# Block 2's first modulation on VectorE during attention, and two norms from one pass of squares

## The chip, the core and the metric

The kernel runs on one core of a Trainium2 chip. A core has a matrix engine (TensorE: PE for matmuls, PEld for its weight loads), a vector engine (VectorE, DVE), an engine for functions of one operand (ScalarE, ACT), a general engine (GpSimd, POOL) and a queue engine (SyncE, SP). DMA transfers are issued on the queues of SP and POOL. The metric is the time of one execution on the device, in microseconds (us).

## What is computed

Two transformer blocks, one after the other, on 512 tokens of width 1024, and 256 context tokens for each. All in float32.

Block 1 (`first_block`, one layer): a modulation from a conditioning vector; a mixer of differential attention (4 heads) and gated linear attention (GLA, 4 heads, forward and backward); then a mixture of experts, 32 experts with two per token. It ends with a norm.

Block 2 (`second_block`, two layers): for each layer a modulation, neighbourhood attention, a gated branch, latent attention, a merge, and a feed-forward part; the context rows go through all of layer 0, and through the keys and values of layer 1. What the change touches:

```python
x = x + gt2 * hier_moe(...)                 # block 1: the experts are added
return rms_norm(x, final_norm_g)            # end of block 1
...
s_c = silu(c); s_ctx = silu(c_ctx)          # block 2
for i in range(2):
    mod = s_c @ w_mod[i] + b_mod[i]         # 1024 x 6144, for the latent rows
    mod_c = s_ctx @ w_mod[i] + b_mod[i]     # the same matrix, for the context rows
    ...
    h  = rms_norm(x, g_norm1[i]) * (1 + sc1) + sh1
    hc = rms_norm(ctx, g_norm1[i]) * (1 + mc[1]) + mc[0]
```

So block 1's last norm is followed directly by block 2's first: two root-mean-square norms behind each other on the same rows.

## The kernel before

Rows lie transposed: eight tiles of 128 features by 512 tokens (256 for context). Nearly all products are done in three passes: every weight chunk of 128x1024 is loaded (`wr`), split into a high part on ACT (`wh`, line 168) and a low part on DVE (`wl`, line 169), and multiplied as high x high, high x low, low x high (lines 193 to 195).

The program is written as generators that yield a cost after each step. `Stream` counts cost divided by its speed, and `weave` takes the next step from the stream with the least count, until its main streams are done; streams in `back` go along. The order in which steps are emitted is a priority: a planner then sets the order of instructions on each engine and queue, and an engine works its own list in order. Buffers come from tags with a fixed number of tiles (line 22): `t2` 35 of 512 columns, `wa` 14 and `raw` 4 of 1024, `hl` 6, `at` 9 of 768.

`run` goes through these stages. The times are those of the profiled execution.

- `front`, 0 to 420 us: block 1's norm, projections, GLA and attention. GLA (`gla`, from about 155 us) is woven with gates, values and the first head's projection. In the back goes `mods`, block 1's own second and third modulation group. Then each head `attend(hd)` is woven with the projection `qk(hd + 1)` of the next one; the fourth begins at about 377 us.
- The fourth head also has `ctx` in the back: block 2's work for the context rows of layer 0, `path(0, 256)`. It begins with `opening`, the first of three groups of layer 0's modulation; the second and third (`later`) run beside it and are drained ahead of `gains(..., 2)`.
- `project` (output projection, to about 545 us), with `ctx` at speed 0.3; `route` (norm, router, slots; to about 612 us), at 0.5.
- `experts`, 612 to 1400 us: 16 pairs, each 13.1 of cost (three yields of 4.2 and one of 0.5), with `ctx` at `CTX_SPEED` 1.65. Weight tiles `we` come on SP's queue, the context path's `wr` on POOL's.
- `combine`, from 1400 us, `ctx` at the same speed: gathers each token's two expert rows, adds them to X (line 1064), takes squares (`stat`: ACT and DVE in turn, POOL adds them up), sums over features by matmuls with ones (`rms`, line 249), takes the reciprocal root in twelve small DVE steps (`rsqrt`), spreads it (`spread`), scales X (line 1072), stores it, and takes squares of the scaled X for the next norm.
- `drain(weave(ctx))`, then `path(0, 512)`: its first norm (`norm_mod`, lines 267 to 280) takes those squares, and the rest of block 2 follows, until the end.

A modulation group in `mods_group` (line 312 on) loads 32 tiles of 128x512 of the matrix and multiplies each with both conditioning vectors in a 128x32 operand (line 327). It then copies the sum, transposes it and adds the bias. Both vectors are served by one matmul.

## Time and profile before

| | us |
|---|---|
| median of 3 runs | 3503.2 (3502.89 to 3504.28) |
| the profiled execution, its own time | 3501.3 |
| its span, first to last instruction | 3499.5 |
| PE busy | 3328.7 (95%) |
| DVE busy | 1692.5 (48%) |
| ACT busy | 1235.7 (35%) |
| POOL busy | 420.9 (12%) |
| mean granted TensorE clock | 0.975 |

Busy shares are of the span. A PE that is busy is not PE at its peak. In the page's slices a digit is the busy share in tenths, and PEclk the granted TensorE clock in tenths of full speed (2.4 GHz; the lower level is 1.2 GHz). In a table by stretch, "44.08 (x120)" is 44.08 us busy with 120 instructions.

### The profile page before, as it was taken

To read this page: it belongs to the slowest core of one execution; us is meant where nothing else is said; L and a number is where in the kernel's file an instruction comes from. 1 tells how busy PE (TensorE), PEld (TensorE's weight loads), DVE (VectorE), ACT (ScalarE), POOL (GpSimd) and SP (SyncE) were. 2 spreads that over 40 slices of the span, in tenths; PEclk is the share of its full clock that TensorE was granted. 3 is DMA by queue.
4 is the path that set the end of the run, shared out by engine and by line. 5 is a ranking of instruction groups with operands and counts; after the bars stand their busy time and mean duration, and the time that the engine had idled before them with its cause. 6 is when DMAs were issued, how large, how long until landed. Compare 5 with 4: busy or idle time off the path is not lost. (4 is left out here: it accounts for less than half of the span.)

```text
span 3499.5 us, 48890 instructions
## 1 busy us (share of the span) xinstructions
PE 3328.7 (95%) x19280; PEld 2520.3 (72%) x19280; DVE 1692.5 (48%) x3173; ACT 1235.7 (35%) x2194; POOL 420.9 (12%) x558
## 2 busy tenths in 40 slices
PE   7999998999999999599999999999999999999998
PEld 4987556665666666596577777888797777778887
DVE  5336545434333333544356746444645466554443
ACT  4214323333323332233344523333334344433332
POOL 1000022112221221300001021000300001010000
PEclk9999999999999999799999999999999999999999
DMA  7341566898899999335731232333433222132332
GB/s 264 90 130 37 192 228 246 325 333 322 333 377 357 380 371 343 138 99 181 242 97 50 68 109 85 109 126 96 145 98 108 81 68 67 43 109 96 97 97 78
DMA packets 197076, 596.03 MB, mean 170 GB/s; under 512 B 32124, under 2 KB 36988, under 8 KB 196845
## 3 DMA queue, kind: packets, MB, share of 16 engines
q1 hardware_dynamic: 157148, 463.36, 38.3%
q0 software_dynamic: 39696, 129.54, 10.4%
q8 instruction: 152, 2.49, 0.3%
q14 instruction: 80, 0.65, 0.1%
HBM read 563.69 MB, written 33.29 MB: 171 GB/s over the span
## 5 line engine op out<-in xcount | busy, mean ns | idle before, releaser
L169 DVE TENSOR_TENSOR wl<-wr,wh 128x1024 fp32r<-128x1024 f32 (+2 forms) x452 | 554.9, 1229 | 570.3 <-ACT wh L168 541.8
L168 ACT ACTIVATE wh<-wr 128x1024 fp32r<-128x1024 f32 (+2 forms) x452 | 473.8, 1049 | 723.5 <-PE mm L194 546.6
L193 PE MATMUL mm<-wh,h 128*128 128x256 f32 (+1 forms) x1104 | 321.1, 291 | 6.6 <-ACT h L278 4.9
L194 PE MATMUL mm<-wl,h 128*128 128x256 f32 (+1 forms) x1104 | 317.7, 288 | 0.0
L195 PE MATMUL mm<-wh,h 128*128 128x256 f32 (+1 forms) x1104 | 317.1, 288 | 0.3 <-DVE h L279 0.2
L193 PE MATMUL mm<-u,wh 128*128 128x512 f32 (+1 forms) x768 | 274.2, 357 | 4.3 <-ACT wh L168 4.2
L193 PE MATMUL mm<-f,wh 128*128 128x512 f32 (+1 forms) x768 | 274.4, 359 | 3.6 <-ACT f L278 3.2
L194 PE MATMUL mm<-f,wh 128*128 128x512 f32 (+1 forms) x768 | 273.6, 357 | 0.0
L195 PE MATMUL mm<-u,wl 128*128 128x512 f32 (+1 forms) x768 | 272.6, 355 | 0.7 <-DVE wl L169 0.7
L195 PE MATMUL mm<-f,wl 128*128 128x512 f32 (+1 forms) x768 | 273.1, 356 | 0.0
L194 PE MATMUL mm<-u,wh 128*128 128x512 f32 (+1 forms) x768 | 272.7, 355 | 0.0
L1020 PE MATMUL gu<-we,xT 128*64 128x512 f32 x1024 | 239.4, 599 | 0.2 <-ACT xT L165 0.2
L193 PEld LDWEIGHTS mm<-wh,h 128*128 128x128 f32 x1104 | 215.9, 196 | 19.5 <-issue 7.3
L195 PEld LDWEIGHTS mm<-wh,h 128*128 128x128 f32 x1104 | 215.0, 195 | 8.4 <-issue 6.4
L194 PEld LDWEIGHTS mm<-wl,h 128*128 128x128 f32 x1104 | 215.9, 196 | 4.8 <-issue 4.0
L193 PE MATMUL pg<-h,wh 128*128 128x512 f32 (+1 forms) x576 | 213.1, 370 | 6.4 <-ACT th L1723 3.8
L194 PE MATMUL pg<-h,wh 128*128 128x512 f32 (+1 forms) x576 | 208.7, 362 | 0.0
L195 PE MATMUL pg<-h,wl 128*128 128x512 f32 (+1 forms) x576 | 208.4, 362 | 0.0
L356 ACT ACTIVATE p<-S,mx 128x768 f32<-128x768 f32 (+2 forms) x192 | 144.5, 755 | 104.9 <-DVE mx L1429 61.4
L193 PEld LDWEIGHTS mm<-u,wh 128*128 128x128 f32 x768 | 145.9, 190 | 32.0 <-issue 7.5
L193 PEld LDWEIGHTS mm<-f,wh 128*128 128x128 f32 x768 | 146.1, 191 | 31.8 <-issue 6.5
L1020 PEld LDWEIGHTS gu<-we,xT 128*64 128x64 f32 x1024 | 71.4, 137 | 129.1 <-issue 121.4
(513 smaller groups left out, 6538.5 us busy)
## 6 DMA issues: line engine op xcount, KB each, us to landing
we<-in_expert_w_gate_dram SPq DMA_DIRECT2D x128, 512.0 KB, 9.5
we<-in_expert_w_up_dram SPq DMA_DIRECT2D x128, 512.0 KB, 11.4
we<-in_expert_w_down_dram SPq DMA_DIRECT2D x128, 512.0 KB, 11.0
wr<-in_ffn_w_dram SPq DMA_DIRECT2D x128, 512.0 KB, 3.7
wr<-in_w_in_dram SPq DMA_DIRECT2D x120, 512.0 KB, 4.0
wr<-in_ffn_w_dram POOLq DMA_DIRECT2D x64, 512.0 KB, 6.9
wr<-in_w_in_dram POOLq DMA_DIRECT2D x58, 512.0 KB, 4.5
wm<-in_w_mod_dram SPq DMA_DIRECT2D x96, 256.0 KB, 4.9
```

Of the source, the lines that this page charges most:

```text
L168: self.nc.scalar.activation(hi, src, AF.Copy)
L169: self.nc.vector.tensor_tensor(lo, src, hi.bitcast(F32), op=OP.subtract)
L193: mm(out, ah, bh, start=i == 0, stop=False)
L194: mm(out, ah, bl, start=False, stop=False)
L195: mm(out, al, bh, start=False, stop=i == n - 1)
L356: self.nc.scalar.activation(p, s, AF.Exp, bias=m, accum_out=sm)
L1020: nc.tensor.matmul(gu[64 * e:64 * e + 64, m * 512:m * 512 + 512], xT[k // 4][:, o:o + 64], w[e][kk], start=k == 0, stop=k == KD - 1)
```

## The change

Layer 0's modulation of block 2 leaves TensorE. `mods2_cols` loads the matrix transposed (`w_mod_t`, laid out on the host; 48 column blocks of 128, in two halves of 512 inputs) and both conditioning vectors as rows repeated on all partitions (`c2_rows`). It makes four rows of silu and computes each column by two multiply-and-sum instructions for each vector on DVE. It is a stream `cols` in the back of GLA and of the first three heads, and is drained ahead of the fourth. `ctx` is then `path(0, 256)` alone, and starts in the fourth head at speed 1.0 (`LAST_SPEED`; 0.5 before); its speed is 1.45 in the experts (1.65 before) and 2.0 in `combine` (1.65 before).

`combine` takes squares of X and of X times the gain `gf`, both on ACT, sums all sixteen tiles by matmuls, and computes both reciprocal roots r and r2 from these sums. X is not scaled there. `path(0, 512)` multiplies its gain by `gf`, norms the unscaled X with r2, and then (`normed`) scales and stores X. What is left of `ctx` is no longer drained ahead of `path(0, 512)` but woven with its first norm.

```diff
-CTX_SPEED = 1.65
+CTX_SPEED = 1.45
+TAIL_SPEED = 2.0
+COL_COST = 2.0
+LAST_SPEED = 1.0
...
     def rms(self, st, n):
         acc, T = self.tp("ss"), n // P
-        for t in range(T):
+        self.sums(acc[:, :T], st)
+        return self.rsqrt(acc[:, :T], T, 1.0 / D)
+
+    def sums(self, acc, st):
+        for t in range(acc.shape[1]):
             for i, sq in enumerate(st):
-                self.nc.tensor.matmul(acc[:, t:t + 1], sq[:, t * P:(t + 1) * P], self.ones[:, :1], start=i == 0, stop=i == 1)
+                self.nc.tensor.matmul(acc[:, t:t + 1], sq[:, t * P:(t + 1) * P], self.ones[:, :1], start=i == 0, stop=i == len(st) - 1)
...
-            later = Stream(rest(), 1.0, False)
-            ctx = [Stream(chain(opening(), self.path(0, 256, before=later))), later]
+            ctx = [Stream(self.path(0, 256))]
         for s in ctx:
-            s.speed = 0.5
+            s.speed = LAST_SPEED
...
-                                     (self.experts(), CTX_SPEED, False), (self.combine(), CTX_SPEED, False)):
+                                     (self.experts(), CTX_SPEED, None), (self.combine(), TAIL_SPEED, None)):
...
-            drain(weave(ctx))
+            self.rest = ctx
...
+        cols = Stream(self.mods2_cols(0, COL_COST) if ctx else iter(()), 1.0, False)
+        drain(weave([Stream(gla(), 1.0, False), Stream(chain(gates(), dv(), qk(0)), 1.2)], [mods, cols]))
         drain(mods.gen)
         for hd in range(4):
+            if hd == 3:
+                drain(cols.gen)
             drain(weave([Stream(attend(hd), 1.0, False), Stream(chain(gate_norm() if hd == 0 else (), qk(hd + 1) if hd < 3 else ()), 1.2)],
-                        ctx if hd == 3 else ()))
+                        ctx if hd == 3 else [cols]))
...
     def combine(self):
...
-            self.stat(ss, m, X[m], 512)
+            for sq, g in ((ss, 1.0), (sg, gf[:, m:m + 1])):
+                sq.append(self.t2("sq"))
+                nc.scalar.activation(sq[-1], X[m], AF.Square, scale=g)
+            yield 1
         del Y
+        acc = self.tp("ss")
+        self.sums(acc[:, :4], ss)
+        self.sums(acc[:, 4:8], sg)
+        yield 1
+        keep = self.t2("keep")
+        r, v, r2 = (keep[:, 4 * i:4 * i + 4] for i in range(3))
+        nc.vector.tensor_copy(r, self.rsqrt(acc[:, :4], 4, 1.0 / D))
+        nc.vector.tensor_tensor(v, r, r, op=OP.mult)
+        nc.vector.tensor_tensor(v, v, acc[:, 4:8], op=OP.mult)
+        nc.vector.tensor_tensor(r2, self.rsqrt(v, 4, 1.0 / D), r, op=OP.mult)
         yield 4
-        r = self.spread(self.rms(ss, 512), 512)
-        yield 8
-        ss = []
+        self.norms = gf, r, r2
+
+    def normed(self, X, norm):
+        nc, (gf, r, _) = self.nc, self.norms
+        yield from norm
+        r = self.spread(r, 512)
         for m in range(KD):
             nc.vector.scalar_tensor_tensor(X[m], X[m], gf[:, m:m + 1], r, op0=OP.mult, op1=OP.mult)
             nc.gpsimd.dma_start(self.xs_dram[0][m], X[m])
-            self.stat(ss, m, X[m], 512)
-            yield 1.5
-        self.ss = ss
+            yield 0.7
...
+    def mods2_cols(self, L, cost):
+        nc = self.nc
+        bt, mod = self.mod2[L]
+        rows = [[self.load(self.at("crow")[:, :512], self.A["c2_rows"][c, h]) for h in range(2)] for c in range(2)]
+        junk = self.t2("junk")
+        for s in rows[0] + rows[1]:
+            nc.scalar.activation(junk, s, AF.Tanh, scale=0.5)
+            nc.vector.scalar_tensor_tensor(s, junk, 1.0, s, op0=OP.add, op1=OP.mult)
+        yield 1
+        for j in range(48):
+            w = [self.load(self.at("wc")[:, :512], self.A["w_mod_t"][j, h]) for h in range(2)]
+            for c in range(2):
+                to, beg = mod[:, j, c:c + 1], bt[:, j:j + 1]
+                for h in range(2):
+                    nc.vector.tensor_tensor_reduce(junk, w[h], rows[c][h], 0.5, beg, OP.mult, OP.add, to)
+                    beg = to
+            yield cost
...
+            if L == 0:
+                nc.vector.tensor_tensor(m["a1"], m["a1"], self.norms[0], op=OP.mult)
+                r = self.norms[2]
...
+        if L == 0 and lat:
+            norm = self.normed(X, norm)
...
+        if L == 0 and lat:
+            norm = chain(weave([Stream(norm, 1.0, False)], self.rest), weave(self.rest))
         yield from norm
...
-        if before:
-            yield from before.gen
...
-    A["w_mod"] = np.stack([modw(x["w_mod_2"][i]) for i in range(2)])
+    A["w_mod"] = modw(x["w_mod_2"][1])
+    A["w_mod_t"] = ca(x["w_mod_2"][0].T.reshape(48, P, 2, 512).transpose(0, 2, 1, 3))
+    A["c2_rows"] = ca(np.repeat(np.stack([x["c_2"][0], x["c_ctx_2"]]).reshape(2, 2, 1, 512), P, 2))
```

## Rows read from the trace of the kernel before

**Rows 1.** The page, its parts 1 and 2 (busy times; 40 slices).
```profile
PE 3328.7 (95%) x19280; PEld 2520.3 (72%) x19280; DVE 1692.5 (48%) x3173; ACT 1235.7 (35%) x2194; POOL 420.9 (12%) x558
...
PE   7999998999999999599999999999999999999998
...
PEclk9999999999999999799999999999999999999999
```

**Rows 2.** Busy time by stretch: length, engines (instructions), PEclk, DMA share, GB/s.
```profile
155.00:272.00 117.00, 115.43 (x856) 94.12 (x855) 44.08 (x120) 23.41 (x50) 3.71 (x4) 1.00 0.36 113
272.00:377.00 105.00, 101.24 (x555) 78.56 (x554) 70.34 (x118) 46.78 (x94) 8.41 (x6) 0.98 0.10 31
377.00:420.00 43.00, 41.05 (x189) 21.03 (x188) 24.50 (x58) 14.17 (x32) 1.86 (x2) 0.92 0.73 242
420.00:545.00 125.00, 120.77 (x482) 60.26 (x480) 53.67 (x121) 28.07 (x44) 22.09 (x29) 0.99 0.73 255
545.00:612.00 67.00, 58.53 (x373) 44.48 (x372) 43.56 (x154) 26.26 (x43) 18.80 (x31) 0.95 0.66 236
612.00:1400.00 788.00, 774.71 (x4855) 503.12 (x4856) 307.87 (x586) 265.30 (x494) 161.83 (x255) 0.99 0.93 349
1400.00:1465.00 65.00, 30.21 (x167) 26.51 (x165) 35.88 (x65) 14.20 (x18) 33.91 (x37) 0.65 0.48 172
```

**Rows 3.** Tile mod alone, 377 to 612 us: busy; one matmul; its loads (min/median/max ns).
```profile
sum 235.00, PE 74.66 PEld 10.10 DVE 2.05; mean PE 24.89 PEld 3.37 DVE 0.68
...
468.56 1.04 PE L327 MATMUL mod<-wm,mod2ss 128*32 128x512 f32 x2
...
L152 SPq DMA_DIRECT2D wm<-in_w_mod_dram x144: 327/328/1339, 377.1 to 1738.3; - x144
```

**Rows 4.** Groups by line: instructions, count | busy us, mean ns | idle before.
```profile
L169 DVE TENSOR_TENSOR dqk<-rx,dqk 128x512 fp32r<-128x512 f32 x8 | 5.5, 685 | 1.2 <-ACT dqk L168 1.2
L711 DVE TENSOR_REDUCE hss<-sq 128x4 f32<-128x512 f32 x4 | 2.5, 673 | 0.0
L169 DVE TENSOR_TENSOR wl<-wr,wh 128x1024 fp32r<-128x1024 f32 x16 | 19.5, 1222 | 6.6 <-ACT wh L168 6.6
...
L1057 DVE SCALAR_TENSOR_TENSOR yr<-yr,cc,yr x4: 1276/1278/1284, 1410.3 to 1422.0; 128x1024 f32<-128x1024 f32 x4
...
L356 ACT ACTIVATION_READ_ACCUMULATOR p<-S,mx 128x1 f32 x192 | 38.2, 199 | 0.0
```

**Rows 5.** PE's waits, 1397 to 1480 us: total, times, longest; two instructions.
```profile
PE ss L249 <- POOL sq L242: 19.1, 2, 13.3
PE rb L209 <- DVE rs L222: 5.0, 2, 2.5
...
1415.28 0.48 DVE L1396 SCALAR_TENSOR_TENSOR xr<-mm,cc,xr 128x256 f32<-128x256 f32 x1 [1.07 <-PE mm L195]
...
452.81 0.50 PE L249 MATMUL ss<-cc,sq 128*128 128x1 f32 x4
```

**Rows 6.** Timeline, 1427 to 1465 us: start, length, engine, instruction [idle before].
```profile
1432.06 0.74 DVE L1064 SCALAR_TENSOR_TENSOR xr<-yT,cc,xr 128x512 f32<-128x512 f32 x1
...
1436.32 3.57 PE L249 MATMUL ss<-cc,sq 128*128 128x1 f32 x16 [5.83 <-POOL sq L242]
...
1443.62 2.06 DVE L1072 SCALAR_TENSOR_TENSOR xr<-xr,cc,rb 128x512 f32<-128x512 f32 x3 [1.35 <-PE rb L209]
...
1456.80 3.57 PE L249 MATMUL ss<-cc,sq 128*128 128x1 f32 x16 [13.29 <-POOL sq L242]
...
1464.02 2.06 DVE L271 SCALAR_TENSOR_TENSOR nt<-xr,cc,rb 128x512 f32<-128x512 f32 x3 [1.27 <-PE rb L209]
```

**Rows 7.** The experts' matmuls (groups by line), and the stretch with most DMA.
```profile
L1020 PE MATMUL gu<-we,xT 128*64 128x512 f32 x1024 | 239.4, 599 | 0.2 <-ACT xT L165 0.2
...
L1039 PE MATMUL py<-we,hT 128*64 128x512 f32 x512 | 116.0, 601 | 0.1
...
1250.00:1300.00 50.00, 49.94 (x319) 32.39 (x316) 17.77 (x26) 16.70 (x28) 8.79 (x14) 1.00 0.99 377
```

More of the change, by code (lines that the diff above doesn't have):

```diff
@@ L379, in run @@
         if two:
-            place = lambda n: self.place(n)
-            first = Stream(self.mods2(0, "t2", (0,), place))
-            def rest():
-                while not first.done:
-                    yield 1
-                yield from self.mods2(0, "t2", (1, 2), place)
-            def opening():
-                while not first.done:
-                    yield first.step()
-            later = Stream(rest(), 1.0, False)
-            ctx = [Stream(chain(opening(), self.path(0, 256, before=later))), later]
+            ctx = [Stream(self.path(0, 256))]
         for s in ctx:
-            s.speed = 0.5
+            s.speed = LAST_SPEED
         if two and not one:
@@ L409, in run @@
                     s.speed = speed
-                drain(weave([Stream(gen, 1.0, held, (lambda: tc.high_priority(PRIOR)) if PRIOR and held is not None and speed != CTX_SPEED else None)], ctx))
+                drain(weave([Stream(gen, 1.0, bool(held), (lambda: tc.high_priority(PRIOR)) if held is not None else None)], ctx))
         if two:
-            drain(weave(ctx))
+            self.rest = ctx
             self.fill = [Stream(self.path(1, 256), FILL_SPEED)]
@@ L728, in gate_norm @@
             yield 0.5
-        mods = Stream(chain(*[self.mods_group(mod, s0, A["w_ada"], g, "at", lambda n: self.place(n)) for g in (1, 2)]), MOD_SPEED, False)
-        self.place = self.dd
-        drain(weave([Stream(gla(), 1.0, False), Stream(chain(gates(), dv(), qk(0)), 1.2)], [mods]))
+        mods = Stream(chain(*[self.mods_group(mod, s0, A["w_ada"], g, "at", self.dd) for g in (1, 2)]), MOD_SPEED, False)
+        cols = Stream(self.mods2_cols(0, COL_COST) if ctx else iter(()), 1.0, False)
+        drain(weave([Stream(gla(), 1.0, False), Stream(chain(gates(), dv(), qk(0)), 1.2)], [mods, cols]))
         drain(mods.gen)
-        self.place = self.mm
         for hd in range(4):
+            if hd == 3:
+                drain(cols.gen)
             drain(weave([Stream(attend(hd), 1.0, False), Stream(chain(gate_norm() if hd == 0 else (), qk(hd + 1) if hd < 3 else ()), 1.2)],
-                        ctx if hd == 3 else ()))
-        self.place = self.dd
+                        ctx if hd == 3 else [cols]))
         def project():
@@ L1045, in combine @@
     def combine(self):
-        nc, ss = self.nc, []
+        nc, ss, sg = self.nc, [], []
         X = self.X = self.load_x(self.xs_dram[0], 512, "xr", "wa")
@@ L1163, in second_start @@
         self.mod2 = [self.mods(A["b_mod"][L], f"mod2{L}") for L in range(2)]
+    def mods2_cols(self, L, cost):
[15 more added lines that the diff above has]
+            yield cost
     def mods2(self, L, tag, groups=range(3), place=None):
         for g in groups:
-            yield from self.mods_group(self.mod2[L], self.s2, self.A["w_mod"][L], g, tag, place)
+            yield from self.mods_group(self.mod2[L], self.s2, self.A["w_mod"], g, tag, place)
     def gains(self, L, c, half):
@@ L1177, in gains, with path @@
                     b2=self.col(mod, 3, c, "b2" + pre), g2=self.col(mod, 5, c, "g2" + pre))
-    def path(self, L, n, side=None, before=None):
+    def path(self, L, n, side=None):
         nc, A = self.nc, self.A
@@ L1191, in path @@
             X, self.X = self.X, None
-            r = self.ss
+            if L == 0:
+                nc.vector.tensor_tensor(m["a1"], m["a1"], self.norms[0], op=OP.mult)
+                r = self.norms[2]
+            else:
+                r = self.ss
         else:
```

1 line of the change is left out of this document (removed).

## The prediction

> **What bounds the kernel now.** The page comes first: TensorE (PE) is busy for 95% of the span, VectorE (DVE) for 48%, and of the slices of PE only one is far below nine tenths, the seventeenth, where PEclk falls too [rows 1]. So this kernel is a queue of matrix work. What shortens it is matrix work taken away or a hole closed; what lengthens it is anything that makes PE wait. The next view cuts the span at the places that the change touches [rows 2]. To be seen there: 155 to 377 us (the gated linear attention, then the first three heads) and 612 to 1400 us (the experts, with block 2's context rows woven in) have PE busy for 96% or more. From 1400 to 1465 us (the combination of the experts) it is busy for 30.2 of 65 us at a granted clock of 0.65. DVE has room between 155 and 272 us (44.1 of 117) and less between 272 and 377 us (70.3 of 105). DMA engines are busy for 0.36 and 0.10 of those two stretches, and for 0.93 of the experts' stretch.
>
> **What the modulation costs today.** Layer 0's three groups are 96 matmuls in 192 records, and between 377 and 612 us they hold PE for 74.7 us [rows 3]. They go one by one, each about 1.04 us for its two records [rows 3], because each waits for its own 256 KB. All of that goes. Its 96 loads don't go: they move ahead, from this stretch into 155 to 377 us, still on SP's queue, at 0.33 us of issue each [rows 3], with four loads of rows added. They bring 25 MB into stretches with 0.10 to 0.36 DMA share, which hides them. On SP's queue, which is in order, the projections' weight loads stand behind them; a load that waits for a buffer holds these up. That cost is in the second rival.
>
> **What the modulation costs afterwards.** 48 columns x 2 vectors x 2 halves = 192 multiply-and-sum instructions of 128x512 on DVE, and four small preparations. The trace has no such instruction. Lower bound: the plain product of two 128x512 tiles, 0.685 us [rows 4]. Near row above it: ScalarE's read-out of a sum takes 0.2 us more [rows 4], so 0.885 if the sum is read out the same way. Upper bound: product and separate sum, 0.685 + 0.673 = 1.36 us [rows 4]. I take 0.80, between the first two, since a product that streams one element at a time can add as it goes.
>
> By the code's own step costs the columns take 1 + 48 x 2 = 97 units: the linear attention's stretch gives about 56 units (27 columns), the three heads 15 each (the other 21). DVE's spare time there is (117 - 44.1) + (105 - 70.3) = 107.6 us [rows 2]. The columns ask for 192 x 0.80 = 154 us. PE's work in both stretches is unchanged and has nothing to give, so the excess is paid in time: **192 x d - 107.6 = +46 us** at d = 0.80; +24 at 0.685; +153 at 1.36. The excess could also vanish: block 2's path is now allowed from the fourth head on, and DVE has 18 us to spare in 377 to 420 and 71 in 420 to 545 [rows 2]; if columns slide there, it falls towards zero. I don't count on it, since they are emitted ahead of the fourth head.
>
> The Trainium skill has a rule against this step: "Vector Engine (DVE) Microarchitecture Reference", section "Points that are easy to get wrong", says that the instruction form with two sources and an accumulator halves its throughput when both sources are in SBUF and not bf16. The nearest row disagrees as far as it goes: scalar_tensor_tensor of two 128x1024 f32 tiles in SBUF takes 1.28 us, the plain product of that size 1.22 [rows 4]; but it sums nothing. By the page, an estimate of d is 0.685 + (1.222 - 0.685) = 1.22 us, the excess 127 us, and the time some 3534 us.
>
> **The hole behind the experts.** After the last context matmul (its result at 1415.3 us) PE waits: 19.1 us for POOL's additions of squares, 5.0 us for the two reciprocal roots [rows 5]. The chain is: additions to X until 1432.8, POOL's adds of squares, sums from 1436.3, root, X scaled from 1443.6, a second set of squares with POOL's adds, sums from 1456.8, root, norm at 1464.0 [rows 6]. Afterwards there are no POOL adds and no second pass: last X, its two squares on ACT, the remaining sums, a root, three small steps, a second root with the spread. A root with its spread takes 3.7 us (1439.9 to 1443.6 [rows 6]), so the norm could start about 1444, 20 us sooner, if PE has the sums' time free. The scaling of X and its eight stores come behind the norm, beside matmuls, where DVE and POOL have room; I cost them at nothing, and at 8 x 2.06 / 3 = 5.5 us [rows 6] if they block DVE's splits.
>
> The larger part is what fills the hole. The context path's steps sum to 403 units. Before: 50 units until the experts begin (its first group of modulation aside), 346 in them (16 x 13.1 x 1.65), 8 in the combination. Now: 15.7 (fourth head) + 13.4 (projection) + 31.8 (routing) = 61, then 16 x 13.1 x 1.45 = 304, leaving 38 units for the combination and the norm. A unit is worth (774.7 - 239.4 - 116.0) / 346 = 1.2 us of PE [rows 2, 7]. So 46 us of matrix work lands where PE now idles for 34.8 us [rows 2], and the same amount less lies in the experts' stretch (42 x 1.2 = 51 us, of which 13 us moved ahead). Work that is only moved changes nothing; what is won is the idle time. I count 25 of 34.8 (10 stay, at the gathers and the roots) and 8 for the clock: 30.2 us of work at a granted 0.65 would be 20 at full clock [rows 2], two of the ten left in doubt: **-33 us**, bounds -43 and 0.
>
> The sums cost PE more: 128 records where 32 stood (16 before each norm), at 0.50 / 4 = 0.125 us [rows 5]: **+12 us**; +21 at the half clock's 3.57 / 16 = 0.22 [rows 6].
>
> **Sum.** -74.7 + 46 - 33 + 12 = -50 us on the span of 3499.5: 3450; with the 1.8 us around the span (3501.3) and the 1.9 by which the median is above the profiled execution, **3453 us**.
>
> **Rivals.**
> 1. *Slower: the multiply-and-sum takes two passes.* For: nothing in the trace sums while it multiplies on DVE, a reduction of 128x512 alone costs as much as the product [rows 4], and the heads' DVE is already 67% busy. Against: the 1.28 us row. Gains are 74.7 + 33 - 12 = 96 us, so the point of decision is 192 d - 107.6 = 96, d = 1.06 us. At d = 1.36 the time is 3453 + 107 = 3560. The page's rule above falls here as well (3534). Chance 0.15.
> 2. *The heads choke on buffers.* Tag "at" has nine; the four rows of the conditioning vectors hold four until the last column, two go to each column, and three are left: one query tile's two p and its pt. Then tiles no longer overlap, and each of a tile's five DVE steps can stand behind one 0.8 us multiply: 12 x 5 x 0.8 = 48 us more, 3501 us. For: nine buffers now let three tiles overlap. Against: tiles follow each other at 105 / 12 = 8.75 us with DVE two thirds busy, so much of a step's wait for DVE is in that time already. Chance 0.13.
> 3. *The experts' weights can't come faster.* That stretch moves 349 GB/s x 788 us = 275 MB [rows 2] and would shrink to 737 us; the 268 MB left to it (42 of 403 units of the path's 63 MB, 122 loads of 512 KB, lie outside) need 364 GB/s. The best 50 us reached 377 [rows 7], but the mean was 349. If 355 is the limit, 755 us, +18: 3471. Chance 0.12.
> 4. *The hole stays.* If the order puts context work ahead of the combination after all, the 33 us don't come: 3486. Chance 0.08.
>
> **How the numbers follow.** The forecast has 0.52, for its own range of 3420 to 3490. Other cases: 0.15 at about 3560, 0.13 at 3501, 0.12 at 3471, 0.08 at 3486. Low end: d = 0.685 (+24), hole -43, gives 3421; a spill of the columns into later room takes away most of that 24: 3405. High end 3530: above it lies most of rival 1 (0.13, with d from about 1.2 on), and a few hundredths lie below 3405. 0.2% of 3503 is 7 us, what can be told from no change: faster means under 3496, slower over 3510. Faster: 0.52 + 0.12 + 0.08 less 0.02 of tails = 0.70. Same: most of rival 2, 0.10. Slower: rival 1, the rest of rival 2 and a tail, 0.20.
>
> **What would show it.** Right: no mod matmul ahead of the experts but block 1's own; the fourth head starting some 46 us later than 377, with DVE near nine tenths busy and PE below it ahead of that; multiply-and-sum at 0.7 to 0.9 us; the first expert matmul at about 612 - 75 + 46 + 14 = 597; context matmuls of the feed-forward part between the combination's transposes and a granted clock near 1 there; the norm of block 2 within 50 us of the last expert. Wrong: a multiply-and-sum above 1.06 us; waits of the heads' ACT or PE for a freed "at" buffer; experts' matmuls waiting for "we" loads; PE idle behind the experts as now.

## The result

The changed kernel takes **3523.6 us** (median of 5 runs, 3519.5 to 3525.5) where the kernel before took 3503.2 (5 runs on the same chip): a ratio of 1.0054, 95% interval 1.0042 to 1.0066. It is half a per cent slower; 3453 was forecast. The profiled execution has a span of 3521.8 us, at a mean granted clock of 0.967 (before: 0.975).

Page of the changed kernel, parts 1 and 2 (the slices are 88 us each):

```profile
PE 3332.4 (95%) x19172; PEld 2556.9 (73%) x19172; DVE 1813.0 (51%) x3552; ACT 1241.3 (35%) x2206; POOL 406.4 (12%) x546
...
PE   7998879899999999899999999999999999999998
...
PEclk9999979899999999899999999999999899999999
```

Beside [rows 1]: the seventeenth slice, the hole behind the experts, has gone from 5 to 8 tenths of PE and from 7 to 8 of the clock, so it is mostly filled, as forecast. New are three lower slices, the fourth to the sixth (264 to 528 us), with the clock at 7 tenths in the sixth. Something was won where it was expected, and something was lost in attention.

The busy time by stretch, cut at landmarks: the first score matmul of attention, the last maximum of head 4, the first norm of the routing, the first expert matmul, the last one, the first norm of block 2. The columns are stretch, length, then busy time of PE, weight loads, DVE, ACT, POOL with instructions, granted clock, DMA share, GB/s. First the kernel before, three of these stretches:

```profile
150.00:272.60 122.60, 120.95 (x898) 99.06 (x898) 46.62 (x127) 25.03 (x53) 3.71 (x4) 1.00 0.36 113
272.60:418.80 146.20, 140.49 (x733) 98.80 (x736) 93.22 (x173) 60.19 (x123) 10.27 (x8) 0.96 0.28 92
1394.30:1464.00 69.70, 35.91 (x211) 31.64 (x207) 36.69 (x65) 15.92 (x19) 35.54 (x40) 0.68 0.48 170
```

The changed kernel, all six:

```profile
150.00:320.40 170.40, 164.57 (x909) 103.25 (x907) 110.42 (x320) 25.15 (x53) 3.64 (x4) 1.00 0.58 182
320.40:517.50 197.10, 158.12 (x744) 123.50 (x745) 170.17 (x409) 65.61 (x135) 18.88 (x20) 0.80 0.31 98
517.50:607.90 90.40, 82.65 (x477) 70.72 (x477) 52.98 (x109) 31.10 (x46) 24.09 (x33) 0.96 0.56 181
607.90:685.40 77.50, 65.64 (x410) 54.48 (x410) 50.29 (x173) 38.10 (x74) 17.43 (x27) 0.87 0.61 218
685.40:1406.50 721.10, 710.05 (x4396) 447.30 (x4397) 270.53 (x512) 230.09 (x429) 147.27 (x231) 1.00 0.96 368
1406.50:1485.30 78.80, 70.05 (x476) 67.17 (x473) 39.30 (x73) 31.84 (x45) 19.18 (x26) 0.83 0.51 170
```

Read as lengths, with those of before at the same landmarks:

| stage | before | after | difference |
|---|---|---|---|
| up to the first score matmul | 272.6 | 320.4 | +47.8 |
| four heads | 146.2 | 197.1 | +50.9 |
| projection | 123.0 | 90.4 | -32.6 |
| routing | 73.5 | 77.5 | +4.0 |
| experts | 779.0 | 721.1 | -57.9 |
| combination, to block 2's norm | 69.7 | 78.8 | +9.1 |
| the rest | 2035.5 | 2036.5 | +1.0 |

**Up to the end of the heads 98.7 us are lost; behind them 76.4 are won.** The prediction's steps, sorted in the same way: +46 for VectorE's excess, -16 for the mod matmuls that leave head 4 (PE 16.1 us on tile mod from 272.6 to 418.8 us before) and +13 for context work that moves ahead into it make +43 ahead; -93 is left behind. The first half was 56 us short, and the experiments are mainly about that; the second was 17 short.

Three views of the changed kernel name suspects. The multiply-and-sum itself, by line (count, busy us, mean ns), is not one of them: 192 of 0.765 us, the second line overlapping the first, and 148.4 us of DVE time together (72.3 of it ahead of the first score matmul, 76.1 in the heads), so d = 0.77 where 0.80 was forecast.

```profile
L1190 DVE CUSTOM_DVE_ANT_0 junk<-wc,crow,cc 128x512 f32<-128x512 f32 x192 | 146.8, 765 | 5.2 <-DMA wc<-in_w_mod_t_dram 4.1
L1190 DVE DVE_READ_ACCUMULATOR2_ANT cc<- 128x1 f32 x192 | 15.7, 82 | 0.0
```

The second view is tile mod. Block 1's own modulation (w_ada, groups 1 and 2: 64 matmuls) runs on PE during the linear attention, in both kernels. Before, 16 records at a time took 1.92 us (timeline; a matmul of f32 leaves two records):

```profile
204.14 1.92 PE L327 MATMUL mod<-wm,mod0ss 128*32 128x512 f32 x16
```

The changed kernel: the same tile, first its busy time by stretch, then its timeline, then what SP's queue waited for from 150 to 320 us (total, times, longest):

```profile
150.00:320.00 170.00, 52.39 (x112) 7.19 (x112) 1.38 (x2) 1.00 0.58 183
```
```profile
202.30 1.05 PE L334 MATMUL mod<-wm,mod0ss 128*32 128x512 f32 x2
...
207.20 1.05 PE L334 MATMUL mod<-wm,mod0ss 128*32 128x512 f32 x2
```
```profile
SPq L155 <- PE mod L334: 58.5, 46, 1.9
SPq L155 <- DVE cc L1190: 42.2, 15, 20.5
```

Two records now take 1.05 us, one column group at a time, and SP's queue waits 46 times for a tile that such a matmul gives back and 15 times for one that a multiply-and-sum gives back. The windows at 150 us don't hold the same matmuls in both kernels (86 records before, 112 after). Over all 192 records of w_ada, group 0 included, tile mod held PE for 33.4 us before and for 72.1 us after (from 0 us on):

```profile
0.00:300.00 300.00, 33.44 (x192) 6.36 (x192) 2.06 (x3) 0.97 0.45 145
```
```profile
0.00:320.00 320.00, 72.12 (x192) 10.54 (x192) 2.07 (x3) 0.98 0.55 178
```

The third view is the chain behind the experts: the 128 sums stand as one block, with PE full and a granted clock of 0.50, and DVE waits for its end (timeline, then stretches):

```profile
1450.96 23.09 PE L257 MATMUL ss<-cc,sq 128*128 128x1 f32 x128
...
1474.09 0.16 DVE L219 TENSOR_SCALAR rs<-ss 128x4 f32<-128x4 f32 x1 [22.45 <-PE ss L257]
```
```profile
1451.00:1456.00 5.00, 5.00 (x47) 5.00 (x45) 0.48 (x1) 0.00 (x0) 0.54 (x1) 0.96 0.62 211
1456.00:1474.00 18.00, 18.00 (x86) 18.00 (x86) 0.00 (x0) 0.00 (x0) 0.00 (x0) 0.50 0.00 1
```

### The profile page after: what moved, and what is told of

The parts are those of the page before. It is cut to its first block, busy times and chain, and to the rows that moved or that the text cites. A ratio compares the mean times of both kernels' runs of the same rounds, so it can differ in the third digit from the quotient of the medians.

```text
span 3521.8 us, 49102 instructions
## 1 busy us (share of the span) xinstructions
PE 3332.4 (95%) x19172; PEld 2556.9 (73%) x19172; DVE 1813.0 (51%) x3552; ACT 1241.3 (35%) x2206; POOL 406.4 (12%) x546
## 5 line engine op out<-in xcount | busy, mean ns | idle before, releaser
L171 ACT ACTIVATE wh<-wr 128x1024 fp32r<-128x1024 f32 (+2 forms) x452 | 473.8, 1049 | 714.3 <-PE mm L197 523.7
L196 PE MATMUL mm<-f,wh 128*128 128x512 f32 (+1 forms) x768 | 274.8, 360 | 4.4 <-ACT f L285 3.2
L196 PE MATMUL mm<-u,wh 128*128 128x512 f32 (+1 forms) x768 | 274.7, 358 | 1.0 <-ACT yr L168 0.9
L196 PEld LDWEIGHTS mm<-f,wh 128*128 128x128 f32 x768 | 146.2, 191 | 34.2 <-issue 8.1
L196 PEld LDWEIGHTS mm<-u,wh 128*128 128x128 f32 x768 | 146.2, 190 | 27.1 <-issue 4.9
```

Source lines behind the costliest of these rows:

```text
L171: self.nc.scalar.activation(hi, src, AF.Copy)
L196: mm(out, ah, bh, start=i == 0, stop=False)
```

## The experiments

Medians stand against the kernel before on the same chip (3503.1 us beside e1 to e4, 3503.9 beside e5 to e8, 3503.2 beside e9 to e11, 3505.3 beside e12). "Ahead" is the start of the last maximum of head 4, the landmark up to which the change lost (418.8 before, 517.5 after); "behind" is the span from there on, against 3080.7 before.

| run | median | ratio (95%) | first score | heads | ahead | behind |
|---|---|---|---|---|---|---|
| changed kernel | 3523.6 | 1.0054 (1.0042 to 1.0066) | 320.4 | 197.1 | 517.5 | -76.4 |
| e1 w_ada in raw | 3488.3 | 0.9959 (0.9948 to 0.9971) | 294.7 | 189.7 | 484.4 | -79.0 |
| e2 one vector | 3453.9 | one run | 292.8 | 154.6 | 447.4 | -76.0 |
| e3 norms only | 3504.7 | 1.0003 (0.9992 to 1.0013) | 274.8 | 146.5 | 421.3 | +2.3 |
| e4 sums spread | 3519.5 | 1.0046 (1.0030 to 1.0062) | 318.2 | 198.9 | 517.1 | -79.0 |
| e5 = e1, rows in t2 | 3479.4 | one run | 289.4 | 180.7 | 470.1 | -73.2 |
| e6 = e1, late columns | 3490.2 | 0.9965 (0.9951 to 0.9979) | 281.2 | 173.9 | 455.1 | -47.1 |
| e7 = e1, sums folded | 3474.4 | 0.9909 (0.9893 to 0.9926) | 297.8 | 189.4 | 487.2 | -93.7 |
| e8 columns only | 3521.9 | 1.0046 (1.0029 to 1.0063) | 319.9 | 197.2 | 517.1 | -76.3 |
| e9 = e1, wide columns | 3495.5 | 0.9980 (0.9970 to 0.9990) | 283.3 | 174.5 | 457.8 | -45.9 |
| e10 = e9, sums folded | 3477.5 | 0.9930 (0.9913 to 0.9948) | 283.2 | 174.5 | 457.7 | -64.3 |
| e11 = e3, sums folded | 3489.0 | 0.9964 (0.9953 to 0.9975) | 274.7 | 146.6 | 421.3 | -14.8 |
| e12 = e5, sums folded | 3459.7 | 0.9861 (0.9841 to 0.9881) | 292.6 | 181.2 | 473.8 | -93.2 |

Each landmark is from one profiled execution. Kernels that are alike up to the heads (changed kernel, e4 and e8; e1 and e7; e5 and e12) differ by up to 3.7 us in "ahead", so smaller differences are not read.

The theory after the result: the loss ahead has two causes, tiles (tag at: nine buffers, of which the rows and the pairs of the transposed matrix now hold most) and the supply of VectorE time. The rival is that it is supply alone.

### e1: the w_ada tiles from another tag

```diff
-self.mods_group(mod, s0, A["w_ada"], g, "at", self.dd) for g in (1, 2)
+self.mods_group(mod, s0, A["w_ada"], g, "raw", self.dd) for g in (1, 2)
```

> The changed kernel with one edit: block 1's own modulation weights (w_ada, column groups 1 and 2) are loaded into the 1024-wide tag raw instead of the tag at, whose nine tiles the four rows of the conditioning vectors and the pairs of the transposed matrix hold. Theory 'tiles' (at tiles became scarce, so the 64 matmuls of w_ada run one by one instead of four column groups at a time): PE's mod time between 150 and 320 us falls from 52.4 us to 12 to 25, the first score matmul comes at 275 to 290 instead of 320.4, and the median falls by 30 to 42 us, to 3481 to 3494. Rival 'supply' (VectorE's multiply-and-sums keep the recurrence of attention from VectorE and hold the stage up): the VectorE work is the same, the first score matmul stays behind 310, and the time stays at 3515 to 3530.

Measured: 3488.3 us, 35 less. Tile mod, 150 to 320 us:

```profile
150.00:320.00 170.00, 18.98 (x112) 3.33 (x112) 1.37 (x2) 0.98 0.66 219
```

52.4 became 19.0 us for the same 112 records (34.9 us for all 192), with the same count of multiply-and-sums. Supply alone would have left the first score matmul behind 310; it came at 294.7. That is outside the 275 to 290 that tiles alone gave too: 22 us over the kernel before remain. One word in the code was worth 35 us, more than the whole change had lost. (A tile of raw is 1024 wide and takes two column groups in one load, so the edit gives both other tiles and larger ones.)

### e2: half of VectorE's new work

```diff
-            for c in range(2):
+            for c in range(1):
                 to, beg = mod[:, j, c:c + 1], bt[:, j:j + 1]
```

(The sums left out are set to zero ahead of the columns.)

> The changed kernel without the 96 multiply-and-sums of the context's conditioning vector (block 2's context modulation is left at zero, so the context rows come out wrong); all loads and all tiles stay. Theory 'supply': half of 147 us of VectorE work is gone, the four heads lose about half of the 51 us that they gained, the stage before the heads loses about half of its 48, and the time is 3470 to 3485. Theory 'tiles' for the stage before the heads: the first score matmul stays at 305 to 320 us, since the four rows and the pairs still hold the tiles; only the heads shrink by 20 to 30, and the time is 3493 to 3505.

Measured: 3453.9 us, below both ranges. The heads shrank from 197.1 to 154.6 us, by 42.5 for 43.0 us of multiply-and-sum less in them (33.2 instead of 76.1). Part of that can be tiles, since the probabilities' waits for a tile (see e5) are gone here too. e12, which has next to no such waits, settles it: its heads are 26.6 us longer than those of e2 (181.2 us) for 26.5 us of DVE work more (158.0). So in the heads supply is the limit, at full price. The stage ahead of them shrank by 27.6, which both theories had put smaller. The likely reason: the tiles are given back by the multiply-and-sums, so half of the work also means tiles back sooner (tile mod: 27.9 us from 150 to 320). The two causes are not told apart there. The stretches of this run, up to the first score matmul and the heads:

```profile
150.00:292.80 142.80, 137.99 (x918) 99.83 (x917) 83.43 (x236) 25.76 (x54) 3.64 (x4) 1.00 0.69 227
292.80:447.40 154.60, 138.31 (x745) 108.74 (x746) 131.49 (x296) 64.75 (x135) 19.21 (x20) 0.90 0.37 116
```

In the heads DVE is idle for 154.6 - 131.5 = 23.1 us. With all the columns it was 197.1 - 170.2 = 26.9 (changed kernel), in e1 27.8; before it was 53.0. So the heads last as long as VectorE's work in them plus 21 to 28 us. About half of that lies in the fourth head, ahead of which the columns are drained. Up to the fourth head's first maximum (382.1 us before, 404.7 here, 474.2 in the changed kernel) DVE idled for 35.5 us before, 10.1 here and 13.3 in the changed kernel. In e1, e9 and e12 it is 14.2, 9.4 and 12.7. So where the columns stand, 9 to 14 of 35.5 us were not filled.

### e5: the rows out of the tag at as well

```diff
-self.load(self.at("crow")[:, :512], self.A["c2_rows"][c, h])
+self.load(self.t2("crow"), self.A["c2_rows"][c, h])
```

> e1_ada_raw with a second edit: the four rows of the conditioning vectors stand in the tag t2 instead of at, so that the four heads find nine at tiles less the pairs in flight instead of five. Theory 'supply' (in the heads VectorE itself is the bound: 95% busy in e1 between 295 and 440 us): the heads, from the first score matmul to the last maximum, stay at 180 to 195 us as in e1 (189.7), time 3480 to 3492. Rival 'tiles in the heads' (the prediction's rival 2, the probabilities wait for freed at tiles): the heads shrink to 155 to 172 us, time 3463 to 3474.

Measured: 3479.4 us in one run, between the two ranges; the heads 9 us shorter than in e1. The waits of the heads say why (S are the scores, p the probabilities, cc what a multiply-and-sum writes). The changed kernel, 290 to 500 us:

```profile
PE S L196 <- ACT p L363: 16.0, 6, 6.4
ACT p L363 <- DVE cc L1190: 15.8, 7, 6.5
```

In e1 these are 14.4 and 5.9 us, and in e5 there is no wait of p for cc any more:

```profile
PE S L196 <- ACT p L363: 1.7, 2, 1.3
```

A probability waited for a tile that a multiply-and-sum held, and the next scores waited for the probability. So the prediction's second rival was there too, at a smaller price. e12 gives the gain with an interval.

### e6: half of the columns later

```diff
-        cols = Stream(self.mods2_cols(0, COL_COST) if ctx else iter(()), 1.0, False)
+        cols = Stream(self.mods2_cols(0, 4.0) if ctx else iter(()), 1.0, False)
...
                 drain(cols.gen)
+                self.late = Stream(self.mods2_cols(0, 2.0, self.crows, range(24, 48)), LATE_SPEED, False)
```

(late is woven into head 4 and the projection; w_ada as in e1.)

> e1_ada_raw with the columns spread: the first 24 of 48 at half the rate before the fourth head, the other 24 beside the fourth head and the projection, where VectorE was about 60% busy. Theory 'supply' (what a column costs depends on how much VectorE time is free in its stage): the first score matmul comes at 272 to 285 us instead of 294.7, the heads shrink from 189.7 to 150 to 170, the projection grows by 0 to 15, and the median is 3450 to 3472. Rival 'the same wherever it stands' (147 us of VectorE work that is only moved behind the heads lengthens the fourth head and the projection by what it gives back before): 3480 to 3495.

Measured: 3490.2, the rival's time. The heads did shrink (189.7 to 173.9) and the first score matmul came 13.5 us sooner, but the projection grew from 90.4 to 119.6 us. The heads and the projection:

```profile
281.20:455.10 173.90, 150.81 (x766) 118.40 (x765) 141.03 (x324) 66.67 (x136) 19.81 (x20) 0.85 0.31 102
455.10:574.70 119.60, 89.04 (x472) 75.94 (x471) 110.28 (x273) 32.73 (x48) 25.37 (x35) 0.85 0.64 209
```

In the projection DVE was 53.0 of 90.4 us busy in the changed kernel; now it is 110.3 of 119.6, and the granted clock fell from 0.96 to 0.85. There was room for 37 us and it was given 57. What the stages up to the last maximum gave back against e1 (29.3 us), the stages behind it took (31.9): of these places none was free.

### e8 and e3: the two parts alone

e8 leaves combine, path and the context path's drain as before; e3 leaves the modulation on TensorE as before and takes combine, normed and the carried-on context path of the change.

> The first part of the change alone: the modulation from the transposed matrix on VectorE, with the combination, the two norms and the context path's end as in the kernel before. If the two parts don't bear on one another it is slower than before by what the whole change lost less what the norms alone lost (20.4 less 1.6 us): 3518 to 3526. If the norms need the shorter context path to pay (the hole is filled by it, and there is less of it now), the columns alone are worse or better by 8 or more: 3530 and more, or 3514 and less.

> The kernel before with the second part of the change alone: both norms behind the experts from one pass of squares, the context path carried on into them, the modulation left on TensorE. The prediction's step (the hole behind the experts is filled, 33 us gained, 12 paid for 128 instead of 32 sum matmuls): 3476 to 3488. Rival 'block of sums' (the 128 one-column matmuls stand as one block of 23 us at half the granted clock, with nothing beside them, and return what the hole gave): 3500 to 3515.

Measured: 3521.9 (+18.0) for the columns, 3504.7 (+1.6, not to be told from nothing) for the norms, 19.6 together against 20.4: the parts add up. Both lie where the additive theory and the rival 'block of sums' had them. The combination up to block 2's norm, e8 and e3:

```profile
1406.80:1483.60 76.80, 55.47 (x382) 51.48 (x378) 56.35 (x86) 27.37 (x37) 42.11 (x49) 0.84 0.61 211
```
```profile
1396.10:1467.10 71.00, 54.58 (x305) 51.24 (x302) 25.61 (x54) 20.13 (x27) 14.29 (x17) 0.68 0.36 126
```

PE's idle time there was 69.7 - 35.9 = 33.8 us before. It is 21.3 in e8, 16.4 in e3, and 8.8 with both. What fills it is not the same. The context path's matmuls that stand there (one of the three passes of each product; count, busy us, mean ns, idle before), in the kernel before, e3 and e8:

```profile
L193 PE MATMUL mm<-u,wh 128*128 128x256 f32 x45 | 13.8, 307 | 4.2 <-ACT wh L168 4.2
```
```profile
L194 PE MATMUL mm<-u,wh 128*128 128x256 f32 x45 | 14.3, 319 | 4.3 <-ACT wh L169 4.3
```
```profile
L196 PE MATMUL mm<-u,wh 128*128 128x256 f32 x64 | 19.6, 309 | 1.0 <-ACT uu L1396 0.8
L196 PE MATMUL mm<-f,wh 128*128 128x256 f32 x38 | 11.0, 288 | 0.6 <-ACT uu L1396 0.6
```
In all three passes that is 135 records before and in e3, and 306 in e8 and in the changed kernel, which has the same groups of 64 and 38. So it is the first part of the change, which holds the context path's lower speed in the experts (`CTX_SPEED`), that brings context work into the hole. In e3 what filled it are the sums: tile ss takes PE 26.5 us where it took 7.2, and PE's other work there is 28.0 us where it was 28.8. And behind the heads e8 has won as much as the whole change (76.3 and 76.4 us): as they were made, the norms brought nothing, with the filled hole or without it.

### e4 and e7: the sums placed elsewhere, and made fewer

e4 issues the four sums of a square right behind it, into one accumulator:

```diff
+                for t in range(4):
+                    nc.tensor.matmul(acc[:, b + t:b + t + 1], sq[:, t * P:(t + 1) * P], self.ones[:, :1], start=m + b + t == 0,
+                                     stop=m == KD - 1, skip_group_check=True)
...
-        self.sums(acc[:, :4], ss)
-        self.sums(acc[:, 4:8], sg)
```

> The changed kernel with one edit: the four sums of each square are issued right behind that square, between the transposes and the context path's matmuls, instead of all 128 in one block behind the last. Theory 'block of sums': the 23 us block of 1451 to 1474 us is gone, the inverse root starts at about 1455 and the first nt of block 2 at about 1465 instead of 1485.3; the median falls by 12 to 20 us, to 3503 to 3512. Rival 'PE is the bound there' (the sums and the displaced context matmuls take the same PE time wherever they stand): the time falls by 0 to 8 us, 3515 to 3524.

Measured: 3519.5, the rival's range; block 2's norm came 5.8 us sooner (1479.5). The sums bunched anyway, only earlier:

```profile
1430.00:1451.00 21.00, 20.72 (x116) 20.52 (x116) 6.42 (x10) 8.81 (x13) 2.59 (x5) 0.61 0.29 91
```

PE is full here too, at 0.61. With the hole filled, a sum costs PE time in either place. e7 therefore takes sums away, by adding the squares up on DVE:

```diff
+    def fold(self, *accs):
+        for a in accs:
+            if len(a) > 2:
+                self.nc.vector.tensor_tensor(a[0], a[0], a.pop(1), op=OP.add)
```

(called for both norms behind each X[m]; two tiles for each norm are left: 32 records stand where 128 stood.)

> e1_ada_raw with the sixteen squares added up on VectorE, which had some 10 us free between 1415 and 1451 and 22 us behind, to two tiles for each norm, so that 16 instead of 128 one-column matmuls stand behind them. Theory 'PE is the bound behind the experts' (the experiment that spread the sums showed PE 16.7 to 20.7 us busy of 18 to 21 wherever the sums stood): 112 sums of 0.11 to 0.21 us leave PE, 12 to 23 us, and the median is 3466 to 3477. Rival 'the chain of gather, squares and root is the bound': 3482 to 3490.

Measured: 3474.4, 13.8 below e1, as the theory had it. The combination of e7, up to block 2's norm:

```profile
1376.70:1437.70 61.00, 50.95 (x380) 48.37 (x377) 46.03 (x85) 32.04 (x45) 17.74 (x26) 0.92 0.63 215
```

61.0 us instead of 78.7 in e1, with the clock at 0.92. e11 does the same to e3:

> e3_norms_only with the squares added up on VectorE as in e7_sums_folded (the modulation on TensorE as before). Theory 'the hole was filled and the 128 sums spent it' (the prediction's 33 us are there, its price of 12 us for the sums was too low): the sums' 20 to 25 us at half clock go and the median is 3480 to 3492. Rival 'there was no 33 us in the hole to win': the median stays at 3497 to 3507.

Measured: 3489.0, 15.7 below e3, and faster than before by 0.36%. The combination of e11, up to block 2's norm:

```profile
1397.00:1453.20 56.20, 34.86 (x209) 31.23 (x206) 32.54 (x66) 20.50 (x27) 14.28 (x17) 0.69 0.45 159
```

The time is in the theory's range, but not for its reason: the hole is not filled here (PE has 34.9 us of work in 209 records, 35.9 us in 211 before). It is shorter, 56.2 us instead of 69.7, because the chain from the last X to the norm is. So the norms' step is worth something once their sums are few. The 96 records more had spent it, with the hole filled (e7, 13.8 us) and without (e11, 15.7 us): they stand for the most part as a block between the last square and the root.

### e9 and e10: the same bytes with less VectorE time

```diff
-            w = [self.load(self.at("wc")[:, :512], self.A["w_mod_t"][j, h]) for h in range(2)]
+            w = self.load(self.H.get("at", self.nm("wc")), self.A["w_mod_t"][j])
...
+                nc.vector.tensor_tensor_reduce(junk, w, rows[c], 0.5, bt[:, j:j + 1], OP.mult, OP.add, mod[:, j, c:c + 1])
...
-T2, WA, RAW, HL, AT = 35, 14, 4, 6, 9
+T2, WA, RAW, HL, AT = 34, 14, 4, 6, 7
```

(at has seven tiles of 1024 columns; the rows and the scratch tile `junk`, which stood in t2, take such tiles too.)

> e1_ada_raw with the multiply-and-sum over a whole row of 1024 at once: 96 instead of 192, the same bytes; the tag at has seven tiles of 1024 instead of nine of 768, t2 34 instead of 35. The rows of before give 1.22 to 1.28 us for VectorE over 1024, so with the read of the sum 96 times 1.30 to 1.36 are 125 to 131 us instead of 148. Theory 'supply' (the heads are as long as VectorE's work in them plus some 25 us): 17 to 23 us of work less, of which the heads give back most and the stage before the heads little: median 3468 to 3480. Rival 'bytes and tiles' (the loads of 25 MB and the tiles that they hold set the pace of the heads): 3484 to 3494.

Measured: 3495.5, above both ranges. A 1024-wide multiply-and-sum takes 1.29 us (mean of 96) and its read 0.08, and all columns together 124.8 us of DVE where they took 147.2 in e1. The heads shrank from 189.7 to 174.5 us, the stage ahead from 294.7 to 283.3, with the same 25 MB. But the edit did a second thing: the first multiply-and-sum started at 68.4 us, where it started at 155.3 in e1. The columns' DVE time in this run, up to 150 us, up to the first score matmul, and in the heads:

```profile
0.00:150.00 150.00, 49.00 (x76) 0.92 0.67 217
150.00:283.30 133.30, 23.18 (x36) 1.00 0.56 192
283.30:457.80 174.50, 52.65 (x80) 0.89 0.30 91
```

So the run doesn't tell shorter work from an earlier start. What the heads show agrees with supply: 13.9 us of columns less in them than in e1 (66.6 there), 15.2 us gained. In the kernel before VectorE is idle for 88.6 of the first 150 us, and the change and e1 have no multiply-and-sum there. Which tiles brought the start forward was not tried.

The gain up to block 2's norm is 24.0 us. But the stages from there on grew from 2033.7 to 2064.2 us, which cost more than that. Fewer and wider tiles in at (and one less in t2) are the only thing changed there, and PE's wait of S for p is 25.2 us behind block 2's norm where e1 has 12.7; where the other 18 went was not traced.

> e9_wide_columns with the squares added up on VectorE as in e7_sums_folded: the two act in different stages, so the 14 us of e7 should add up with e9's gain: 10 to 16 us below e9_wide_columns, 3454 to 3469. If the later stages take the gain back (the context path's end becomes late instead): within 5 us of e9_wide_columns.

Measured: 3477.5, 18.1 below e9, a little more than the 10 to 16 expected (the range of times, 3454 to 3469, was missed because e9's own had been). The fold adds up with it, and most of the 30 us behind stay: 2062.4 us from block 2's norm on, 2036.5 in e7.

### e12: both kinds of tiles and the fold

The edits of e1, e5 and e7 together.

> All that the runs found for the columns and the tail together: w_ada in raw, the four rows in t2 (as in e5_ada_raw_rows_t2) and the squares added up on VectorE (as in e7_sums_folded), nothing taken from the blocks behind. If tiles were a second, smaller limit of the heads (e5 had 14 us less up to block 2's norm than e1), the median is 8 to 14 us below e7_sums_folded: 3460 to 3467. Rival 'the look at e5 showed chance': 3470 to 3477, as e7_sums_folded.

Measured: **3459.7 us, 1.4% faster than the kernel before** and 64 us faster than the change as it was made; 14.7 below e7, so e5 was no chance; the gain is at the upper end of what was expected (8 to 14). Up to the first score matmul, the heads, the combination:

```profile
150.00:292.60 142.60, 135.90 (x960) 104.42 (x958) 125.81 (x359) 28.94 (x61) 3.75 (x4) 0.98 0.72 242
292.60:473.80 181.20, 152.19 (x748) 118.69 (x748) 158.04 (x379) 65.30 (x136) 19.38 (x20) 0.83 0.31 100
1363.20:1424.60 61.40, 50.80 (x380) 48.47 (x377) 46.07 (x86) 31.95 (x45) 18.18 (x26) 0.92 0.63 213
```

In the first two stretches DVE is idle for 16.8 and 23.1 us. In the heads VectorE's work is the bound (see e2). Ahead of them that isn't shown: there PE is busy for 135.9 of 142.6 us. And some 5 of the 20 us by which the first score matmul still comes later than before arise ahead of 150 us, where no column runs yet: PE is busy for 122.5 of the first 150 us, in e1 for 122.4, in the changed kernel for 126.9 and before for 127.3, so they came with w_ada's move to raw.

The heads, cut at the first maximum of head 4, in the kernel before and in e12:

```profile
272.60:382.10 109.50, 105.64 (x577) 81.80 (x576) 74.05 (x123) 47.85 (x97) 8.41 (x6) 0.98 0.14 39
382.10:418.80 36.70, 34.84 (x157) 17.00 (x160) 19.17 (x50) 12.34 (x27) 1.86 (x2) 0.91 0.72 247
```
```profile
292.60:430.60 138.00, 117.95 (x580) 90.42 (x580) 125.35 (x291) 47.83 (x98) 11.43 (x10) 0.88 0.33 103
430.60:473.80 43.20, 34.24 (x169) 28.27 (x169) 32.69 (x89) 17.48 (x39) 7.94 (x10) 0.67 0.25 87
```

Head 4 thus begins 48.5 us later than before in e12, and 92.1 in the changed kernel. Behind that point the fourth head takes 6.5 us longer in e12 and 6.6 in the changed kernel, though no column stands in it. Its mod matmuls are gone (PE 16.7 us from 382.1 us on before, 42 records), but the context path's products stand there in their place (14.5 us in 47 records in the changed kernel; the second line is one of their three passes):

```profile
L327 PE MATMUL mod<-wm,mod2ss 128*32 128x512 f32 x42 | 16.7, 671 | 0.2 <-DMA wm<-in_w_mod_dram 0.2
```
```profile
L196 PE MATMUL mm<-wh,h 128*128 128x256 f32 x16 | 5.0, 320 | 0.0
```

## Why the prediction was wrong

**The direction was wrong because of one step: "192 x d - 107.6 = +46 us".** It was to be all that the columns cost. Up to the first maximum of head 4 the changed kernel lost 92.1 us.

*"PE's work in both stretches is unchanged"* failed, since the sum put the shared tiles at nothing and they ran short. The matmuls of w_ada share the tag at with the new rows and columns, and went from 33.4 to 72.1 us of PE when four column groups at a time became one. The prediction knew that three of nine tiles were left, but it priced that (second rival) for the heads' probabilities alone and not for the other user of the tag in the stage ahead. From the changed kernel to e12, which relieves both users of the shortage and takes nothing of VectorE's work away, head 4 begins 43.6 us sooner: 27.8 of it ahead of the first score matmul, 15.8 in the heads. That is nearly all of the error in this step, for e12 stands at +48.5. (e12 also folds the sums, but these lie behind.) The rival's own price for the heads, 48 us, was three times too high; it let all 60 steps wait for one multiply-and-sum each, where seven waits of 2.3 us for a tile were seen.

The Trainium skill, "TensorE: Matmul & The Clock Gate", section "Part 3: Packing small matmuls — row/col tiling", says that matmuls with few output rows run at the same time when each has its own column group. The trace agrees, with 16 records in 1.92 us in the kernel before; it also shows what that needs, since where each waits for a tile the same matmuls take 1.05 us for two records.

*All of VectorE's idle time was taken as usable*: this was wrong too, but another error hid it. From 150 us to head 4's first maximum DVE was idle for 111.4 us before, and in e12 for 29.5 us still (16.8 and 12.7), where the prediction left none. But DVE's busy time in these stretches rose by 130.5 us (120.7 to 251.2), not by 154: with the overlap of neighbours that is 0.68 us for each multiply-and-sum, not 0.80 (by its own line d is 0.77). The two errors cancel, so that +46 comes out at +48.5 once tiles are there is luck in good part. In the heads a likely reason for what stays idle is that the chain of score, maximum, probability, transpose and product goes back and forth between the engines; no run tests that. Ahead of the heads PE is busy for 93% and more (e1, e5, e12), so what bounds that stage stays open.

*The fourth head* was to be 3 us shorter by the prediction's count (16 us of mod matmuls leave, 13 us of context work come), and is 6.6 longer, with a granted clock of 0.65 instead of 0.91 (36.3 us of PE in 43.3, 34.8 in 36.7 before). That it is as long in e2 and e12 (42.7 and 43.2) shows that neither columns nor tiles do it.

A reading that nothing was worked out from: the prediction has each of layer 0's mod matmuls wait for its own 256 KB; from 377 to 612 us the kernel before names 7 such waits, 2.7 us together.

**Behind the heads 17 us are missing.** -93 forecast, -76.4 measured. The mod matmuls' 58.6 us went from there. The hole looks as forecast: 25 of 34.8 us of idle time were to be filled, 33.8 - 8.8 = 25.0 were, and the granted clock rose from 0.68 to 0.83 (the prediction's 8 us for that were not measured by themselves). But part of what filled it are the sums themselves: tile ss took PE 23.1 us instead of 7.2, 16 more where the prediction had 12 (it took 0.125 us per sum, the price at full clock; at 0.22 it had 21), and in one block ahead of the root. e8, with the norms as before, has -76.3: the second part of the change, as it was made, brought nothing. Taking 96 of the 128 records away gave 13.8 us back (e7), and e12 has -93.2. So the sums' price was the term that was too small.

**The signs named ahead.** d between 0.7 and 0.9: right. Context matmuls among the combination's transposes with the clock near 1: right up to 1451 us. DVE near nine tenths busy and PE below it ahead of the fourth head: right (0.92 and 0.79 from 320 to 470 us). The fourth head some 46 us later: 92, and 48.5 in e12. First expert matmul at about 597: 685.4. Block 2's norm within 50 us of the last expert: 78.8, because of the block of sums and the second root behind it (61.4 in e12). Of the signs of a wrong forecast, the wait for a freed at tile is the one that showed: on SP's queue (58.5 and 42.2 us) and on ACT (15.8 us).

**The other rivals.** The first fell: a multiply-and-sum took 0.765 us, near the product's 0.685 and far from product and sum, 1.36. By the Trainium skill's rule ("Vector Engine (DVE) Microarchitecture Reference", "Points that are easy to get wrong") it would have been 1.22 us, an estimate; the trace has 0.765 for two f32 sources in SBUF, with 0.08 us for the read of the sum, mostly overlapped. The instruction is a custom one in the trace, so the rule for the form that the page names is not tested by it. That the 3534 us of this rival lie near the 3523.6 measured is chance. The third fell: the experts took 721.1 us at 368 GB/s, where it gave 755. The fourth fell with the hole filled.

**What stays open**: the 18 us of e9's rest that no wait named, and what bounds the stage ahead of the heads in e12. The context path's speeds were not varied by themselves. And that the usable idle time is bound to the order in which columns are queued among the heads' steps on DVE was not tried; e6 moved columns between stages, not within one.

## What to carry to other kernels

When a step takes buffers of a shared tag, list every user of that tag in the stages concerned and ask of each how many tiles it needs at once to run as it does now; a user that isn't touched by the edit can lose most. Work moved to an engine that is idle half of the time isn't free up to the last idle microsecond: where columns stood among the heads' steps, 9 to 14 of 35.5 us were not used, and beyond that it was paid in full (e2 to e12: 26.6 us of time for 26.5 of work). And price small instructions by where they stand: the 96 records of sums more stood as a block between the last square and the root, and cost 14 us with PE's hole filled and 16 us without.

## What the runs showed of the hardware

- The granted clock fell to 0.50, the lower level, while PE's records show no idle time at all: 86 records of one-column matmuls filled 18.00 of 18.00 us from 1456 us on; from 1446 to 1451 us, with 256-column matmuls, it was 1.00. A record took 0.106 us at 0.96 (47 in 5 us) and 0.209 at 0.50. The Trainium skill, "TensorE: Matmul & The Clock Gate", section "Why this matters for your kernels", warns of idle gaps between matmuls; here the records show none.
- The multiply-and-sum costs a little more than the plain product of the same size: 0.765 against 0.685 us at 512, 1.29 (e9) against 1.22 at 1024 [rows 4]. 96 of double width took 124.8 us of DVE where 192 took 147.2 (e1).
- In the heads PE's granted clock was lower the longer PE was idle: it went from 0.96 before to 0.80 with the columns and 0.90 with half of them (e2), with PE idle for 5.7, 39.0 and 16.3 us. Whether a part of the 51 us comes from matmuls at the lower clock is not shown.
